# A decoder layer's weight blocks: six hand-divided places of one tile instead of a buffer for each block

## The chip, the cores and the metric

The kernel runs on one core of one Trainium2 chip. The metric is the device time of one execution in microseconds (us); below 2080.77 us is the median of three runs of the kernel as it was (2077.95 to 2080.8).

## The reference, cut to what matters

One decoder layer over 528 tokens (16 learned ones ahead of 512), all in float32, width 2048:

```python
n = rmsnorm(h, g_mix);  p = n @ w_in                  # 2048 -> 6144: q, k, v, b, c, u
o = concat(stick_breaking_attention(q, k, v), b * causal_conv(c * u))   # each group normed
h = h + o @ w_out                                     # 2048 -> 2048
n2 = rmsnorm(h, g_ffn)
h = h + (silu(n2 @ w_gate) * (n2 @ w_up)) @ w_down    # 2048 -> 5632 -> 2048
return h[:, 16:]
```

Nothing of what is computed changes. The change touches only where the weights of `w_out`, `w_gate`, `w_up` and above all `w_down` stand in the core's SBUF, and so when they are loaded.

## The kernel before, in words

**Precision.** A float32 product is made of three matmuls in the faster type `fp32r`: a weight block is split into `hi` (ACT casts it, L613) and `lo` (DVE subtracts `hi` from the block, L614), the activations likewise, and TensorE (PE) adds hi by hi (L706), hi by lo (L707) and lo by hi (L708) into one PSUM bank. One matmul is 128x128 weights by 256 tokens.

**Seven products for eight.** From the gate and up projections on, the work goes in *pairs*: a pair is a 2x2 arrangement of weight blocks `11`, `12`, `21`, `22` (two output tiles by two halves of the contraction), multiplied by a 2x2 arrangement of activation blocks with seven block products instead of eight. The weights of the seven are, in order: `11`; `t1 = 11 + 12`; `t2 = t1 + 22`; `22`; `t3 = 12 + 22`; `21`; and the final `t2 = t2 + 21`. DVE makes the sums: L620 makes t1 and t3, L654 and L627 add to t2, which stands in t1's buffer. There are 72 pairs: 44 for gate and up (0 to 43; 8 weight tiles of 128 to a block), 4 double pairs of `w_down`'s first chunk (44 to 47; again 8 tiles), and 24 pairs of `w_down`'s other three chunks (48 to 71, eight to a chunk; 6 tiles to a block, so 128x768). A pair of the last kind is 7 products of 18 matmuls, 126 in all. The activation blocks of these chunks stand in a ring of buffers that POOL's queue fills from DRAM (`ring<-fd`).

**The banks.** The products of a pair go to three PSUM banks in the order x, z, x, z, x, y, x (`pair_product`). After the fifth product DVE takes its result out of bank x (L741, into `d`), and the seventh product, which goes to bank x again, may not start before. The sixth product, to bank y, lies between: 18 matmuls for pairs 48 to 71.

**The loads.** SP's queue holds the weight loads, strictly in order; each waits until its buffer is free. Before the change each of the four blocks has one buffer of 128x1024 (`b11`, `b12`, `b21`, `b22`, L591), so `22` of pair i+1 can be loaded only when `22` of pair i has been split. Each load is issued by `load_quad(i + 1, q)` beside the last instruction that reads the same block of pair i. Two further buffers of that size serve t1 and t3 (`sum`), and three double ones hold hi and lo of the split blocks (`s`): three products are prepared at a time. All of it takes 48 KB of each partition, before the change and after it.

**The order.** The program is recorded with a scheduler that moves instructions by priority and by what they depend on; `prepare_pair` runs at high priority, ahead of the products by two. DVE, ACT and SP each work strictly in the order that it made.

Of the kernel before, what the change touches and what calls it, by code (L numbers as in the profile page):

```python
# [9 lines left out]
F32 = mybir.dt.float32  # L10
F32R = mybir.dt.float32r
# [4 lines left out]
P = 128  # L16
# [6 lines left out]
KT = D // P  # L23
FT = FF // P
# [9 lines left out]
def hybrid_layer(ctx: ExitStack, tc: tile.TileContext, xT, w_in, w_out, w_gu, w_down, vecs, out):  # L34
# [12 lines left out]
    def open_pool(name, bufs=1, **kw):  # L47
        return tc.alloc_tile_pool(name=name, bufs=bufs, reuse_waits="tile", **kw)
# [513 lines left out]
    sw = open_pool("sw", side="right")  # L562
    acc_h = hpool.tile([P, SEQ], F32, name="acc_h")
    hpool.tile([P, 24], F32, name="pad_h")
    pairs = []
# [17 lines left out]
    quads, sums, split_w, used = {}, {}, [], [0]  # L583
    S_AHEAD = 2
    ORDER = ("21", "11", "12", "22")
    WIDE = 2 * KT - 2

    def load_quad(i, q):
        if i < len(pairs):
            n, srcs = pairs[i]  # L590
            quads[i, q] = sw.tile([P, 8 * P], F32, tag=f"b{q}", name=f"b{q}_{i}")[:, : n * P]  # L591
            src, dst = srcs[("11", "12", "21", "22").index(q)], quads[i, q]
            if len(src.shape) == 3:
                dst = dst.rearrange("p (t c) -> p t c", t=2)
            nc.sync.dma_start(dst, src)

    wide = []

    def load_wide():

        i = len(wide)
        q = ORDER[(i + 2) % 4]
        if i < WIDE:
            wide.append(sw.tile([P, 8 * P], F32, tag=f"b{q}", name=f"wide{i}"))
            nc.sync.dma_start(wide[i], w_out[OUT_TILES[1 + i // 2], i % 2])
        else:
            wide.append(None)
            load_quad(0, q)

    def split_quad(src, n):  # L610
        t = sw.tile([P, 2, 8 * P], F32R, tag="s", bufs=S_AHEAD + 1, name=f"s{len(split_w)}")
        hi, lo = (t[:, i, : n * P] for i in range(2))
        sc.copy(hi, src)  # L613
        ve.tensor_tensor(lo, src, hi.bitcast(F32), ALU.subtract)  # L614
        split_w.append((hi, lo))

    def add_quads(i, name, a, b):
        n = pairs[i][0]
        sums[name] = sw.tile([P, 8 * P], F32, tag="sum", bufs=2, name=f"{name}_{i}")[:, : n * P]
        ve.tensor_tensor(sums[name], a, b, ALU.add)  # L620

    def add_t3(i, b):
        add_quads(i, "t3", b["12"], b["22"])
        load_quad(i + 1, "12")

    def add_last(i, b):
        ve.tensor_tensor(sums["t2"], sums["t2"], b["21"], ALU.add)  # L627
        load_quad(i + 1, "21")


    FIRST_ORDER = (5, 0, 1, 2, 3, 4, 6)
# [1 line left out]
    def prepare_pair():  # L633
        if len(split_w) < WIDE:
            with tc.high_priority():
                split_quad(wide[len(split_w)], 8)
                load_wide()
            return
        i, s = divmod(len(split_w) - WIDE, 7)
        if i == len(pairs):  # L640
            return
        n = pairs[i][0]
        if i == 0:
            s = FIRST_ORDER[s]
        with tc.high_priority():
            b = {q: quads[i, q] for q in ("11", "12", "21", "22") if (i, q) in quads}
            if s == 0:
                split_quad(b["11"], n)
                add_quads(i, "t1", b["11"], b["12"])
                load_quad(i + 1, "11")  # L650
            elif s == 1:
                split_quad(sums["t1"], n)
                sums["t2"] = sums["t1"]
                ve.tensor_tensor(sums["t2"], sums["t2"], b["22"], ALU.add)  # L654
                if i:
                    add_t3(i, b)
            elif s == 2:
                split_quad(sums["t2"], n)
                if not i:
                    add_t3(i, b)  # L660
            elif s == 3:
                split_quad(b["22"], n)
                load_quad(i + 1, "22")
            elif s == 4:
                split_quad(sums["t3"], n)
            elif s == 5:
                split_quad(b["21"], n)
                if i:
                    add_last(i, b)
            else:  # L670
                if not i:
                    add_last(i, b)
                split_quad(sums["t2"], n)

    def prepare_ahead(n):
        while len(split_w) < min(WIDE + 7 * len(pairs), used[0] + n):
            prepare_pair()
# [96 lines left out]
    for _ in range(4):  # L774
        load_wide()
# [11 lines left out]
    for i, j in enumerate(OUT_TILES):  # L787
# [8 lines left out]
        half, k = divmod(j, 8)  # L796
# [285 lines left out]
```

## Time and profile before

| | |
|---|---|
| median of 3 runs | 2080.77 us (2077.95 to 2080.8) |
| the profiled execution | 2082.13 us, its span 2080.4 us |
| PE busy | 2057.9 us, 99% of the span |
| VectorE (DVE) busy | 1628.2 us, 78% |
| ScalarE (ACT) busy | 1016.4 us, 49% |
| loads of `w_down` of 128x768 | 96, 384.0 KB each, median 3.9 us from issue to landing |
| loads of the activation ring, 768.0 KB | 42, median 14.1 us |
| granted TensorE clock | 0.998 of full speed on average |

A line of the profile names a line of the kernel, an engine, an operation, and what it writes and reads without buffer numbers: `t<-b,b` is a sum of two loaded blocks, `s<-b,s` a split of one, `d<-x,sides` the reading out of bank x. "Idle before" is the time in which the engine stood still ahead of an instruction, with what ended it. PE's matmuls overlap: each is shown as 0.28 us long, but the next one starts about 0.11 us later. SPq and POOLq are the queues of transfers that SP and POOL issue.

### The profile page before, as it was taken

To read this page: it belongs to the slowest core of one execution; us is meant where nothing else is said; L and a number is where in the kernel's file an instruction comes from. 1 tells how busy PE (TensorE), PEld (TensorE's weight loads), DVE (VectorE), ACT (ScalarE), POOL (GpSimd) and SP (SyncE) were. 2 spreads that over 40 slices of the span, in tenths; PEclk is the share of its full clock that TensorE was granted. 3 is DMA by queue.
4 is the path that set the end of the run, shared out by engine and by line. 5 is a ranking of instruction groups with operands and counts; after the bars stand their busy time and mean duration, and the time that the engine had idled before them with its cause. 6 is when DMAs were issued, how large, how long until landed. Compare 5 with 4: busy or idle time off the path is not lost.

```text
span 2080.4 us, 39146 instructions
## 1 busy us (share of the span) xinstructions
PE 2057.9 (99%) x16086; PEld 1983.3 (95%) x16086; DVE 1628.2 (78%) x2133; ACT 1016.4 (49%) x1522; POOL 368.3 (18%) x499
## 2 busy tenths in 40 slices
PE   9999999999999999999999999999999999999999
PEld 8899999999998888999999999999999999999999
DVE  7877777433336668999898888988988977878888
ACT  7666565322224434555555555555555554444443
POOL 0111111010003544111011011111110233131210
PEclk9999999999999999999999999999999999999999
DMA  5222222222235666546555465465555999696765
GB/s 194 63 82 73 80 72 82 85 97 93 92 112 163 186 185 224 160 139 194 155 166 164 146 174 158 137 174 166 146 171 151 290 336 340 149 334 155 206 149 110
DMA packets 144116, 330.41 MB, mean 159 GB/s; under 512 B 12400, under 2 KB 62064, under 8 KB 143936
## 3 DMA queue, kind: packets, MB, share of 16 engines
q1 hardware_dynamic: 67456, 212.50, 32.1%
q0 software_dynamic: 76480, 115.40, 21.8%
q8 instruction: 126, 2.06, 0.4%
q14 instruction: 54, 0.44, 0.1%
HBM read 260.74 MB, written 67.11 MB: 158 GB/s over the span
## 4 chain that ended last, share of the span: by engine, by line
PE 90%; DVE 4%; DMA 4%; ACT 1%; issue 1%; SPq 0%; POOL 0%; DVEq 0%; ACTq 0%; POOLq 0%
PE x L706 10%; PE x L708 10%; PE x L707 10%; PE z L706 5%; PE z L707 5%; PE z L708 5%; DMA b<-w_down 3%; PE po L685 3%; PE po L686 3%; PE po L687 3%; PE y L707 2%; PE y L708 2%; PE y L706 2%; DVE s L614 2%; PE pu L177 1%; PE pc L177 1%
## 5 line engine op out<-in xcount | busy, mean ns | idle before, releaser
L613 ACT CAST s<-t 128x1024 fp32r<-128x1024 f32 (+1 forms) x288 | 283.2, 983 | 372.8 <-PE z L708 165.6
L614 DVE TENSOR_TENSOR s<-t,s 128x1024 fp32r<-128x1024 f32 (+1 forms) x288 | 327.4, 1137 | 101.6 <-ACT s L613 99.4
L708 PE MATMUL x<-f,s 128*128 128x256 f32 x1408 | 388.2, 276 | 3.2 <-DVE s L614 3.2
L707 PE MATMUL x<-f,s 128*128 128x256 f32 x1408 | 388.3, 276 | 1.5 <-DMA f<-fx 1.3
L706 PE MATMUL x<-f,s 128*128 128x256 f32 x1408 | 388.1, 276 | 0.2 <-ACT f L187 0.2
L613 ACT CAST s<-b 128x1024 fp32r<-128x1024 f32 (+1 forms) x216 | 212.4, 983 | 159.7 <-PE x L708 141.0
L708 PEld LDWEIGHTS x<-f,s 128*128 128x128 f32 x1408 | 265.2, 188 | 3.4 <-DVE s L614 3.4
L707 PEld LDWEIGHTS x<-f,s 128*128 128x128 f32 x1408 | 265.1, 188 | 1.9 <-DMA f<-fx 1.5
L706 PEld LDWEIGHTS x<-f,s 128*128 128x128 f32 x1408 | 265.0, 188 | 0.7 <-ACT f L187 0.4
L614 DVE TENSOR_TENSOR s<-b,s 128x1024 fp32r<-128x1024 f32 (+1 forms) x216 | 245.8, 1138 | 2.6 <-ACT s L613 2.0
L142 DVE TENSOR_TENSOR wlo<-raw,whi 128x512 fp32r<-128x512 f32 (+1 forms) x198 | 139.9, 710 | 126.5 <-ACT whi L141 125.9
L898 POOL DMA_DIRECT2D fd<-s x147 | 103.7, 922 | 693.4 <-DVE s L188 676.9
L141 ACT CAST whi<-raw 128x512 fp32r<-128x512 f32 (+1 forms) x198 | 121.0, 614 | 182.3 <-PE pu L175 65.5
L706 PE MATMUL z<-f,s 128*128 128x256 f32 x704 | 193.8, 275 | 0.7 <-ACT sides L733 0.7
L707 PE MATMUL z<-f,s 128*128 128x256 f32 x704 | 193.8, 275 | 0.2 <-DVE f L188 0.2
L708 PE MATMUL z<-f,s 128*128 128x256 f32 x704 | 193.7, 275 | 0.0
L620 DVE TENSOR_TENSOR t<-b,b 128x1024 f32<-128x1024 f32 (+1 forms) x144 | 166.0, 1153 | 22.9 <-DMA b<-w_down 17.6
L706 PE MATMUL x<-ring,s 128*128 128x256 f32 x608 | 169.2, 278 | 7.8 <-DVE d L741 7.8
L708 PE MATMUL x<-ring,s 128*128 128x256 f32 x608 | 168.8, 278 | 0.5 <-DVE s L614 0.5
L707 PE MATMUL x<-ring,s 128*128 128x256 f32 x608 | 168.7, 277 | 0.0
L706 PEld LDWEIGHTS z<-f,s 128*128 128x128 f32 x704 | 132.2, 188 | 0.9 <-ACT sides L733 0.9
L707 PEld LDWEIGHTS z<-f,s 128*128 128x128 f32 x704 | 132.2, 188 | 0.4 <-DVE f L188 0.4
(349 smaller groups left out, 5581.6 us busy)
## 6 DMA issues: line engine op xcount, KB each, us to landing
b<-w_gu SPq DMA_DIRECT2D x176, 512.0 KB, 3.9
raw<-w_in SPq DMA_DIRECT2D x92, 512.0 KB, 3.3
fd<-s POOLq DMA_DIRECT2D x147, 256.0 KB, 5.3
b<-w_down SPq DMA_DIRECT2D x96, 384.0 KB, 3.9
ring<-fd POOLq DMA_DIRECT2D x42, 768.0 KB, 14.1
wide<-w_out SPq DMA_DIRECT2D x30, 512.0 KB, 3.7
out_T<-d POOLq DMA_DIRECT2D x54, 256.0 KB, 4.6
b<-w_down SPq DMA_DIRECT2D x16, 512.0 KB, 7.9
```

The costliest lines, as they stand in the source:

```text
L141: sc.copy(hi[:, :c], raw)
L142: ve.tensor_tensor(lo[:, :c], raw, hi[:, :c].bitcast(F32), ALU.subtract)
L613: sc.copy(hi, src)
L614: ve.tensor_tensor(lo, src, hi.bitcast(F32), ALU.subtract)
L620: ve.tensor_tensor(sums[name], a, b, ALU.add)
L685: pe.matmul(ps, hi[:, kk], ah, start=k == 0, stop=False)
L686: pe.matmul(ps, hi[:, kk], al, start=False, stop=False)
L687: pe.matmul(ps, lo[:, kk], ah, start=False, stop=k == 7)
L706: pe.matmul(p, hi[:, kk], act[:, 0, k], start=start and j == k == 0, stop=False, skip_group_check=skip)
L707: pe.matmul(p, hi[:, kk], act[:, 1, k], start=False, stop=False, skip_group_check=skip)
L708: pe.matmul(p, lo[:, kk], act[:, 0, k], start=False, stop=k == n - 1, skip_group_check=skip)
L898: gp.dma_start(fd[c][s][:, :, k], t[:, :, i])
```

## The change

All blocks that are loaded, and the two sums, now stand in one tile `sw_in` of 128x6144; the split blocks in a second one, `sw_split`, of the same size. Both are divided by hand.

* Where a block has 8 tiles (pairs 0 to 47) `sw_in` has six places of 128x1024: four for the blocks, two for the sums, as before.
* Where it has 6 (pairs 48 to 71) the same tile has eight places of 128x768: the sums have places 6 and 7, and the blocks go round the **six** places 0 to 5, in the order 11, 12, 22, 21 of pair 48, then 11, 12 of pair 49, and so on.
* The two sums exchange places in every second pair (`(name == "t3") ^ i % 2`): t1 of a pair takes the place that t3 of the pair before had. Before, the pool gave t1 whichever of its two buffers came free first, which was the same one.
* A load is issued when a place comes free, so it is now that of the block two further on (`load_next`). Two more loads are issued when the six places start.

For pairs 48 to 71 this is when a load may be issued, counted in instructions of DVE's order (17 to a pair):

| block | issued before, after | issued now, after | how much earlier |
|---|---|---|---|
| 22 of pair i+1 | split of 22 of pair i | split of 11 of pair i | 9 |
| 21 of pair i+1 | split of 21 of pair i | t3 of pair i | 14 |
| 11 of pair i+1 | split of 11 of pair i | split of 22 of pair i-1 | 8 |
| 12 of pair i+1 | t3 of pair i | split of 21 of pair i-1 | 3 |

First place: SP's queue, the loads for pairs 48, 49 and the first two of 50 (`b12_48` is block 12 of pair 48; a name in the waits is a counter that the load waits for, DVE's or that of an earlier load). Before:

```order
L595 DMA b12_48_18992<-w_down 128x768 [waits DMAHW2_49,DVE_49]
L595 DMA b11_48_18959<-w_down 128x768 [waits DMAHW7_49,DMAHW3_49,DVE_49]
L595 DMA b22_48_19061<-w_down 128x768 [waits DMAHW4_49,DVE_49]
L595 DMA b21_48_19120<-w_down 128x768 [waits DMAHW5_49,DVE_49]
L595 DMA b12_49_19213<-w_down 128x768 [waits DMAHW6_49,DVE_49]
L595 DMA b11_49_19180<-w_down 128x768 [waits DMAHW7_49,DVE_49]
L595 DMA b22_49_19283<-w_down 128x768 [waits DMAHW0_49,DVE_49]
L595 DMA b21_49_19330<-w_down 128x768 [waits DMAHW1_49,DVE_49]
L595 DMA b12_50_19405<-w_down 128x768 [waits DMAHW2_49,DVE_49]
L595 DMA b11_50_19378<-w_down 128x768 [waits DMAHW3_49,DVE_49]
```

and now, all of them into `sw_in`:

```order
L608 DMA sw_in_6909<-w_down 128x768 [waits DMAHW3_49,DVE_49]
L608 DMA sw_in_6909<-w_down 128x768 [waits DMAHW7_49,DMAHW2_49]
L608 DMA sw_in_6909<-w_down 128x768 [waits DMAHW4_49,DVE_49]
L608 DMA sw_in_6909<-w_down 128x768
L608 DMA sw_in_6909<-w_down 128x768 [waits DMAHW5_49,DVE_49]
L608 DMA sw_in_6909<-w_down 128x768
L608 DMA sw_in_6909<-w_down 128x768 [waits DMAHW6_49,DVE_49]
L608 DMA sw_in_6909<-w_down 128x768 [waits DMAHW7_49,DVE_49]
L608 DMA sw_in_6909<-w_down 128x768 [waits DMAHW0_49,DVE_49]
L608 DMA sw_in_6909<-w_down 128x768 [waits DMAHW1_49,DVE_49]
```

They are now 11, 12, 22, 21 of pair 48, then 12, 11, 22, 21 of pair 49, and 11, 12 of pair 50; three of the first six no longer wait for DVE on their own account, since the load ahead of them has waited for it already.

Second place: DVE where the places of 128x1024 give way to those of 128x768 (`z47` and `x47` are banks z and x of pair 47). Before:

```order
L614 TENSOR_TENSOR s363_19088<-t3_47_18990,s363_19088 128x1024
L620 TENSOR_TENSOR t1_48_19178<-b11_48_18959,b12_48_18992 128x768
L614 TENSOR_TENSOR s364_19116<-b21_47_18899,s364_19116 128x1024
L737 SCALAR_TENSOR_TENSOR d_first_18335<-z47_19028,d_first_18335 128x512
L614 TENSOR_TENSOR s365_19147<-t1_47_18957,s365_19147 128x1024
L620 TENSOR_TENSOR t3_48_19211<-b12_48_18992,b22_48_19061 128x768
L741 SCALAR_TENSOR_TENSOR d_first_18335<-x47_19029,d_first_18335 128x512
L614 TENSOR_TENSOR s366_19175<-b11_48_18959,s366_19175 128x768
L744 TENSOR_TENSOR d_first_18335<-y47_19027,sides_8227 128x512
```

and now (L637, L643, L762, L766 and L769 are the former L614, L620, L737, L741 and L744; x3 means three in a row):

```order
L637 TENSOR_TENSOR sw_split_6910<-sw_in_6909,sw_split_6910 128x1024 x3
L762 SCALAR_TENSOR_TENSOR d_first_17695<-z47_18349,d_first_17695 128x512
L637 TENSOR_TENSOR sw_split_6910<-sw_in_6909,sw_split_6910 128x1024
L643 TENSOR_TENSOR sw_in_6909<-sw_in_6909 128x768
L637 TENSOR_TENSOR sw_split_6910<-sw_in_6909,sw_split_6910 128x768
L643 TENSOR_TENSOR sw_in_6909<-sw_in_6909 128x768
L766 SCALAR_TENSOR_TENSOR d_first_17695<-x47_18350,d_first_17695 128x512
L637 TENSOR_TENSOR sw_split_6910<-sw_in_6909,sw_split_6910 128x768
L769 TENSOR_TENSOR d_first_17695<-y47_18348,sides_8161 128x512
```

The sum t1 of pair 48 stood two instructions ahead of the read-out of bank z (L737); its new place overlaps both old places of sums, so it now stands behind the last split of pair 47. Between the read-outs of bank z and bank x there were a split and a sum, and now there are two of each. From pair 49 on DVE's order is what it was.

PE's order is the same instruction for instruction, and so is POOL's. On ACT the first casts of pair 1 are exchanged (block 22 is cast one ahead of t2, since the places of the split blocks now go round in a fixed order), and in the output projection one cast of 128x256 stands behind the weights' cast instead of ahead of it; DVE's splits of these follow. Each half of a split block now has a place of its own, so 232 of the 504 splits on DVE wait for PE as well as for ACT's cast, where they waited for ACT alone (or with a load).

```diff
--- before.py
+++ after.py
@@ -585,15 +585,38 @@
     ORDER = ("21", "11", "12", "22")
     WIDE = 2 * KT - 2
 
+
+    QUADS = ("11", "12", "22", "21")
+    SIX = FT + KT // 4
+    sw_in = sw.tile([P, 6 * 8 * P], F32, name="sw_in")
+    sw_split = sw.tile([P, 6 * 8 * P], F32R, name="sw_split")
+
+    def w_place(t, n, i):
+        return t[:, i * n * P : (i + 1) * n * P]
+
+    def quad_place(i, q):
+        m = QUADS.index(q)
+        return w_place(sw_in, pairs[i][0], m if i < SIX else (4 * (i - SIX) + m) % 6)
+
     def load_quad(i, q):
         if i < len(pairs):
             n, srcs = pairs[i]
-            quads[i, q] = sw.tile([P, 8 * P], F32, tag=f"b{q}", name=f"b{q}_{i}")[:, : n * P]
+            quads[i, q] = quad_place(i, q)
             src, dst = srcs[("11", "12", "21", "22").index(q)], quads[i, q]
             if len(src.shape) == 3:
                 dst = dst.rearrange("p (t c) -> p t c", t=2)
             nc.sync.dma_start(dst, src)
 
+    def load_next(i, q):
+
+        m = QUADS.index(q)
+        if i < SIX:
+            load_quad(i + 1, q)
+            if i + 1 == SIX and m == 3:
+                load_quad(SIX + 1, QUADS[0])
+        else:
+            load_quad(i + 1 + (m + 2) // 4, QUADS[(m + 2) % 4])
+
     wide = []
 
     def load_wide():
@@ -601,31 +624,31 @@
         i = len(wide)
         q = ORDER[(i + 2) % 4]
         if i < WIDE:
-            wide.append(sw.tile([P, 8 * P], F32, tag=f"b{q}", name=f"wide{i}"))
+            wide.append(quad_place(0, q))
             nc.sync.dma_start(wide[i], w_out[OUT_TILES[1 + i // 2], i % 2])
         else:
             wide.append(None)
             load_quad(0, q)
 
     def split_quad(src, n):
-        t = sw.tile([P, 2, 8 * P], F32R, tag="s", bufs=S_AHEAD + 1, name=f"s{len(split_w)}")
-        hi, lo = (t[:, i, : n * P] for i in range(2))
+        k = len(split_w) % (S_AHEAD + 1) * 2
+        hi, lo = (w_place(sw_split, n, k + i) for i in range(2))
         sc.copy(hi, src)
         ve.tensor_tensor(lo, src, hi.bitcast(F32), ALU.subtract)
         split_w.append((hi, lo))
 
     def add_quads(i, name, a, b):
         n = pairs[i][0]
-        sums[name] = sw.tile([P, 8 * P], F32, tag="sum", bufs=2, name=f"{name}_{i}")[:, : n * P]
+        sums[name] = w_place(sw_in, n, (4 if n == 8 else 6) + ((name == "t3") ^ i % 2))
         ve.tensor_tensor(sums[name], a, b, ALU.add)
 
     def add_t3(i, b):
         add_quads(i, "t3", b["12"], b["22"])
-        load_quad(i + 1, "12")
+        load_next(i, "12")
 
     def add_last(i, b):
         ve.tensor_tensor(sums["t2"], sums["t2"], b["21"], ALU.add)
-        load_quad(i + 1, "21")
+        load_next(i, "21")
 
 
     FIRST_ORDER = (5, 0, 1, 2, 3, 4, 6)
@@ -647,7 +670,7 @@
             if s == 0:
                 split_quad(b["11"], n)
                 add_quads(i, "t1", b["11"], b["12"])
-                load_quad(i + 1, "11")
+                load_next(i, "11")
             elif s == 1:
                 split_quad(sums["t1"], n)
                 sums["t2"] = sums["t1"]
@@ -660,7 +683,7 @@
                     add_t3(i, b)
             elif s == 3:
                 split_quad(b["22"], n)
-                load_quad(i + 1, "22")
+                load_next(i, "22")
             elif s == 4:
                 split_quad(sums["t3"], n)
             elif s == 5:
@@ -671,6 +694,8 @@
                 if not i:
                     add_last(i, b)
                 split_quad(sums["t2"], n)
+                if i + 1 == SIX:
+                    load_quad(SIX + 1, QUADS[1])
 
     def prepare_ahead(n):
         while len(split_w) < min(WIDE + 7 * len(pairs), used[0] + n):
```

## The prediction

> **What bounds the kernel now.** I read the page's busy shares first, then who PE waits for.
>
> ```profile
> span 2080.4 us, 39146 instructions
> PE 2057.9 (99%) x16086; PEld 1983.3 (95%) x16086; DVE 1628.2 (78%) x2133; ACT 1016.4 (49%) x1522; POOL 368.3 (18%) x499
> ...
> PE x L706 <- DVE d L741: 7.8, 5, 2.7
> PE x L708 <- DVE s L614: 3.7, 2, 3.2
> ```
>
> PE works through the whole span, so only its pace and its waits count. By far the longest sum of waits is the one for L741, the read-out of bank x: five times, 7.8 us. PE's timeline shows where they are, with the first matmul of pair 48, the first of pair 66 and the last of pair 71 beside them:
>
> ```profile
> 1721.29 0.28 PE L706 MATMUL x<-ring,s 128*128 128x256 f32 x1
> ...
> 1748.77 0.36 PE L706 MATMUL x<-ring,s 128*128 128x256 f32 x1 [0.80 <-DVE d L741]
> ...
> 1764.50 0.35 PE L706 MATMUL x<-ring,s 128*128 128x256 f32 x1 [1.16 <-DVE d L741]
> ...
> 1838.06 0.36 PE L706 MATMUL x<-ring,s 128*128 128x256 f32 x1 [1.87 <-DVE d L741]
> ...
> 1869.87 0.35 PE L706 MATMUL x<-ring,s 128*128 128x256 f32 x1 [1.34 <-DVE d L741]
> ...
> 1958.52 0.55 PE L706 MATMUL x<-ring,s 128*128 128x256 f32 x1 [2.68 <-DVE d L741]
> ...
> 1990.73 0.28 PE L706 MATMUL x<-ring,s 128*128 128x256 f32 x1
> ...
> 2076.30 0.28 PE L708 MATMUL x<-ring,s 128*128 128x256 f32 x1
> ```
>
> All five lie in pairs 48 to 71, the very pairs for which the change adds places. What this stage loses follows from counts. The last six pairs have 6 x 126 = 756 matmuls, 755 intervals in 2076.30 - 1990.73 = 85.57 us: 0.1133 us each, 14.28 us a pair. All 24 pairs have 3023 intervals, 342.6 us at that pace; they took 2076.30 - 1721.29 = 355.0 us. **12.4 us** are lost.
>
> DVE's timeline and the chain of waits say to what. In the chain's rows (start, length) the load's start is its issue and its end its landing:
>
> ```profile
> 1820.94 0.95 DVE L614 TENSOR_TENSOR s<-b,s 128x768 fp32r<-128x768 f32 x1
> ...
> 1827.99 0.95 DVE L614 TENSOR_TENSOR s<-b,s 128x768 fp32r<-128x768 f32 x1
> ...
> 1833.02 0.96 DVE L614 TENSOR_TENSOR s<-t,s 128x768 fp32r<-128x768 f32 x1 [0.39 <-ACT s L613]
> 1836.62 0.96 DVE L620 TENSOR_TENSOR t<-b,b 128x768 f32<-128x768 f32 x1 [2.65 <-DMA b<-w_down]
> 1837.49 0.42 DVE L741 SCALAR_TENSOR_TENSOR d<-x,sides 128x256 f32<-128x256 f32 x1
> ...
> 1740.89 6.34 DMA b<-w_down
> 1756.58 6.39 DMA b<-w_down
> 1828.97 7.55 DMA b<-w_down
> 1861.83 6.51 DMA b<-w_down
> 1948.62 8.36 DMA b<-w_down
> ...
> DVE t L620 <- DMA b<-w_down: 14.3, 9, 3.5
> DMA to landing us min/median/max: 3.0/3.3/9.3
> ```
>
> Take the third stall. The split of block 22 of pair 55 ends at 1828.94; block 22 of pair 56 is issued at 1828.97 into its buffer and lands at 1836.52. The sum t3 = 12 + 22 stood ready to start at 1833.98, when the split ahead of it ended, and waits 2.65 us for it. L741 needs nothing of that load, but stands behind the sum in DVE's order, and PE's seventh product behind L741. So the load had 5.0 us, and where the ring's transfers run beside it it takes 6.3 to 8.4. All five PE stalls follow one of these five loads. The median of 3.3 us shows why the other pairs do not stall.
>
> A part of the 12.4 us comes after the stalls:
>
> ```profile
> core 0: us, PE busy (x) PEld busy (x) DVE busy (x) ACT busy (x) POOL busy (x), PEclk, DMA share, GB/s
> 1793.00:1807.00 14.00, 14.00 (x126) 14.00 (x125) 12.45 (x18) 6.65 (x10) 1.71 (x2) 1.00 0.68 152
> 1836.00:1852.00 16.00, 14.13 (x110) 13.97 (x109) 12.78 (x17) 5.82 (x9) 6.13 (x8) 0.89 1.14 374
> ...
> 1839.08 0.42 PE L707 MATMUL x<-ring,s 128*128 128x256 f32 x1
> ```
>
> The waits as shown sum to 7.85 us; PE's matmuls overlap, so from one start to the next each costs 0.28 - 0.11 = 0.16 us more, 8.7 us for five. The other 3.7 us are matmuls at half clock behind the two long stalls (0.42 us long instead of 0.28, granted clock 0.89 over the 16 us around the one; 0.11 x 16 = 1.8 us of clock missing, twice at the most) and slightly slow ones behind each stall.
>
> [...]
>
> **The change part by part.**
>
> *The loads ahead.* Block 22 is now issued behind the split of block 11 of the pair before, which ends at 1821.89 in the rows above: 7.1 us before 1828.97. It has 12.1 us until its sum instead of 5.0. The longest landing in this stage is 9.3 us. The other blocks had more time already (11 instructions of DVE or more against 6) and get more. So L620 waits for no load here, L741 is on time, and the stalls go with their half clock: -12.4 us. Bounds: -12.4 is all that the stage loses, no more can be gained; if under the ring's transfers landings grew beyond 12.1 us for the worst two, the stalls of 1.87 and 2.68 would stay with their clock, and -12.4 would be -5. I take the whole, since a grown landing must add 2.8 us to the longest seen. PE's next limit is its own pace, which no edit touches.
>
> *The seam at pair 47.* Here two more instructions stand ahead of the read-out of bank x.
>
> ```profile
> 1715.68 0.96 DVE L620 TENSOR_TENSOR t<-b,b 128x768 f32<-128x768 f32 x1
> 1716.56 0.68 DVE L741 SCALAR_TENSOR_TENSOR d_first<-x,d_first 128x512 f32<-128x512 f32 x1
> 1717.16 0.95 DVE L614 TENSOR_TENSOR s<-b,s 128x768 fp32r<-128x768 f32 x1
> ...
> 1716.05 0.84 ACT L613 CAST s<-b 128x768 fp32r<-128x768 f32 x1 [1.66 <-PE x L708]
> 1718.57 0.28 PE L706 MATMUL x<-first,s 128*128 128x256 f32 x1
> ```
>
> The split now ahead of it waits for ACT's cast, which ends at 1716.89; t1 takes DVE's time from 1715.68 to 1716.64 in the meantime. Then the split to 1717.9, t3 to 1718.8, L741 (0.68) to 1719.5. PE wants bank x at 1718.57, so it stalls about **+0.9 us**, once. Bounds 0 (if PE runs late there) and +1.6 (its wait is under 1.87, so I count no clock, but a load that lands late at the seam would add to it; 0.7 is room for that).
>
> *The exchanged sums and fixed rounds.* t1 of the next pair keeps the place that came free, so DVE's order from pair 49 on is the old one: 0. Had it a fixed place, t1 would wait for the last split.
>
> *232 more waits on DVE.* The place that a split's lo half goes to was last read by PE before ACT's cast could begin, so PE is done long before. If one did end last, it would cost the 0.10 us that lie between the landing at 1836.52 and L620 at 1836.62. Cover is DVE's idle time: 14.0 - 12.45 = 1.5 us in 14 us of a quiet stretch, and 1.75 to 2.2 in a gate pair of 19.05:
>
> ```profile
> 1200.00:1219.05 19.05, 19.05 (x171) 19.05 (x170) 16.81 (x20) 9.71 (x13) 4.22 (x6) 1.00 0.82 216
> 1219.05:1238.10 19.05, 19.05 (x171) 19.05 (x170) 17.29 (x21) 10.25 (x13) 1.16 (x3) 1.00 0.32 103
> ```
>
> Seven in a pair are 0.7 us at the most: 0. Without that cover 232 x 0.10 = +23 us.
>
> *Casts and splits exchanged* at pair 1 and in the output projection: one cast and one split ahead of another, 0.98 + 1.14 = 2.1 us by the page's rows, under a product of 24 matmuls, 2.72 us:
>
> ```profile
> L613 ACT CAST s<-t 128x1024 fp32r<-128x1024 f32 (+1 forms) x288 | 283.2, 983 | 372.8 <-PE z L708 165.6
> L614 DVE TENSOR_TENSOR s<-t,s 128x1024 fp32r<-128x1024 f32 (+1 forms) x288 | 327.4, 1137 | 101.6 <-ACT s L613 99.4
> ```
>
> I take 0, with -1 to +1 for it.
>
> *Sum.* -12.4 + 0.9 = -11.5. The profiled execution took 2082.13 us (span 2080.4 and 1.7 around it): 2070.6. It lies 1.4 above the median of the runs shown, 2080.77, from which the same gain gives 2069.3. I predict **2070 us**.
>
> **The rivals.**
>
> 1. *The ring comes late instead.* Weight loads issued earlier share the transfer engines with the ring's transfers, and PE, no longer held up, reaches the ring's blocks sooner. For it: 374 GB/s in the window around the third stall. Against: the list of PE's waits has no row for the ring, the bytes are the same, and most of a chunk's ring blocks are loaded several pairs ahead. Price: the two long stalls' worth comes back at the chunk seams, half the gain: 2070 + 6 = 2076. [...]
> 2. *The change does not do what it says*: an SP queue in strict order could hold an early load behind one whose place is not free. In the table of issues the places come free in the queue's order (splits of 21, t3, splits of 11, splits of 22 in turn), which speaks against it. Then the stalls stay and the seam is added: 2080.8 + 0.9 = 2081.7.
> 3. *Slower: DVE's added waits.* For it: 232 of them, on the engine whose lateness stalls PE today. Against: the idle time quoted. It decides once seven of them use up DVE's 1.5 us in a pair, 0.2 us each; if all their 23 us fell on the path, 2070 + 23 = 2093.
>
> **How the numbers follow.** The forecast has 74%; the ring 12%; no effect 8%; DVE's waits 6%. Its own range is 2066 (the fastest run of before, 2077.95, less 12.4) to 2074 (seam +1.6, casts +1, a short stall left). The range of 8 in 10 takes in the ring and ends short of no effect: 2066 to 2077.5. This kernel can be told from no change by about 0.2%, 4.2 us, so faster means under 2076.6: the forecast and two thirds of the ring's case, 0.82; same, the rest of the ring's and most of no effect, 0.11; slower, DVE's waits and the tail of no effect, 0.07.
>
> **What would show it.** Right: in pairs 48 to 71 no wait of PE for the read-out of bank x except one of about 0.8 us as shown, at the end of pair 47; no wait of the sums for `w_down` over 0.2 us; first to last matmul of these pairs 343 us; no window there with a granted clock under 1.00. Wrong: PE waits named after the ring's transfers (rival 1), sums still waiting for loads issued no earlier than today (rival 2), splits on DVE that PE ends (rival 3). A pace other than 0.1133 us per matmul in these pairs, from weights at other addresses, would make the whole sum wrong, and no row here prices that.

## The result and the profile after

The changed kernel takes 2065.91 us (median of 4 runs, 2065.38 to 2068.78), the kernel before 2079.36 us on the same chip (2075.76 to 2080.8): ratio **0.9939**, 95% interval 0.9926 to 0.9952, that is 13.5 us less by the medians. The forecast was 2070. The profiled execution took 2065.55 us.

The page of the changed kernel, and the list of what PE waits for (us in total, times, longest), from its top row to the one row left for the read-out of bank x (L766, the former L741):

```profile
span 2063.9 us, 39364 instructions
PE 2050.4 (99%) x16086; PEld 1977.2 (96%) x16086; DVE 1629.1 (79%) x2133; ACT 1017.7 (49%) x1522; POOL 368.8 (18%) x499
...
PE x L733 <- DVE sw_split L637: 2.2, 2, 1.7
...
PE x L731 <- DVE d_first L766: 0.3, 1, 0.3
```

The row of 7.8 us is gone. PE's timeline at the seam of pair 47, the first matmul of pair 48 and the last of pair 71:

```profile
1713.73 0.28 PE L733 MATMUL y<-first,sw_split 128*128 128x256 f32 x1
1714.29 0.35 PE L731 MATMUL x<-first,sw_split 128*128 128x256 f32 x1 [0.28 <-DVE d_first L766]
...
1717.12 0.28 PE L731 MATMUL x<-ring,sw_split 128*128 128x256 f32 x1
...
2059.73 0.28 PE L733 MATMUL x<-ring,sw_split 128*128 128x256 f32 x1
```

Pairs 48 to 71 take 2059.73 - 1717.12 = **342.61 us** instead of 355.01: 12.40 us less, PE's pace from end to end. DVE's timeline at the place of the former third stall, the windows of the whole stage and around that place, and the waits and landings of the blocks:

```profile
1827.19 0.96 DVE L643 TENSOR_TENSOR sw_in<-sw_in 128x768 f32<-128x768 f32 x1
1828.07 0.42 DVE L766 SCALAR_TENSOR_TENSOR d<-x,sides 128x256 f32<-128x256 f32 x1
```

```profile
core 0: us, PE busy (x) PEld busy (x) DVE busy (x) ACT busy (x) POOL busy (x), PEclk, DMA share, GB/s
1717.12:2059.80 342.68, 342.68 (x3026) 342.68 (x3024) 302.01 (x404) 158.23 (x239) 63.80 (x78) 1.00 0.80 213
1826.00:1842.00 16.00, 16.00 (x143) 16.00 (x142) 14.22 (x19) 7.19 (x12) 6.12 (x8) 1.00 1.12 374
```

```profile
DVE sw_in L643 <- DMA sw_in<-w_down: 0.8, 2, 0.5
...
DMA to landing us min/median/max: 3.0/4.0/10.1
```

The transfers are as dense as before (374 GB/s) and the slowest load even slower, 10.1 us from issue to landing (9.3 before). No sum notices: t3 runs without a wait and L766 right behind it. The two waits of 0.8 us together lie ahead of pair 48.

The 16.57 us between the last matmuls (2076.30 and 2059.73) are 12.40 of this stage and 4.17 ahead of it. The 4.17 add up from four places: 1.36 won in the program's first 14 us, far ahead of the part that the change touches; 1.07 lost near 802 us, where the changed kernel waits longer for activations; 4.4 won from there to 833 us, in pairs 0 and 1; and 0.5 lost between pairs 1 and 48, of which 0.44 is the seam. Most of the 4.4 belongs to one wait: the third matmul (lo by hi) of pair 1's first product waited 1.5 us longer before than after, and 1.6 us were lost at half clock behind it (3.41 us from 821.63 us on). PE's timeline of the kernel before, and then of the changed one:

```profile
820.15 0.38 PE L708 MATMUL x<-f,s 128*128 128x256 f32 x1 [3.25 <-DVE s L614]
```

```profile
817.19 0.39 PE L733 MATMUL x<-f,sw_split 128*128 128x256 f32 x1 [1.74 <-DVE sw_split L637]
```

Ahead of the split that PE waited for stands the sum t3 of pair 1, which waited 1.77 us for a load of gate weights before and 0.57 us in the changed kernel. The forecast gives pairs 0 and 1 no more than 1 us either way; how far the difference belongs to the change is taken up after the experiments.

### The profile page after: what moved, and what is told of

It is laid out like the page before. It is cut to its first block, busy times and chain, and to the rows that moved or that the text cites. A ratio compares the mean times of both kernels' runs of the same rounds, so it can differ in the third digit from the quotient of the medians.

```text
span 2063.9 us, 39364 instructions
## 1 busy us (share of the span) xinstructions
PE 2050.4 (99%) x16086; PEld 1977.2 (96%) x16086; DVE 1629.1 (79%) x2133; ACT 1017.7 (49%) x1522; POOL 368.8 (18%) x499
## 4 chain that ended last, share of the span: by engine, by line
PE 96%; DVE 2%; DMA 1%; ACT 0%; issue 0%; SPq 0%; POOL 0%; DVEq 0%; ACTq 0%; POOLq 0%
PE x L733 11%; PE x L731 11%; PE x L732 11%; PE z L731 6%; PE z L732 6%; PE z L733 6%; PE y L733 3%; PE y L731 3%; PE y L732 3%; PE po L712 3%; PE po L710 3%; PE po L711 3%; PE pu L177 2%; PE pc L177 2%; PE pv L173 2%; PE pu L173 1%
## 5 line engine op out<-in xcount | busy, mean ns | idle before, releaser
L636 ACT CAST sw_split<-sw_in 128x1024 fp32r<-128x1024 f32 (+1 forms) x534 | 527.0, 989 | 552.4 <-PE z L732 166.7
L637 DVE TENSOR_TENSOR sw_split<-sw_in,sw_split 128x1024 fp32r<-128x1024 f32 (+1 forms) x534 | 615.0, 1152 | 96.9 <-ACT sw_split L636 94.0
L733 PE MATMUL x<-f,sw_split 128*128 128x256 f32 x1408 | 387.3, 275 | 1.7 <-DVE sw_split L637 1.7
L732 PE MATMUL x<-f,sw_split 128*128 128x256 f32 x1408 | 387.3, 275 | 1.3 <-DVE f L188 1.3
L731 PE MATMUL x<-f,sw_split 128*128 128x256 f32 x1408 | 387.2, 275 | 0.2 <-ACT f L187 0.2
L733 PEld LDWEIGHTS x<-f,sw_split 128*128 128x128 f32 x1408 | 264.3, 188 | 1.9 <-DVE sw_split L637 1.9
L732 PEld LDWEIGHTS x<-f,sw_split 128*128 128x128 f32 x1408 | 264.3, 188 | 1.5 <-DVE f L188 1.5
L731 PEld LDWEIGHTS x<-f,sw_split 128*128 128x128 f32 x1408 | 264.3, 188 | 0.5 <-ACT f L187 0.4
L731 PE MATMUL z<-f,sw_split 128*128 128x256 f32 x704 | 193.7, 275 | 0.6 <-ACT sides L758 0.6
L732 PE MATMUL z<-f,sw_split 128*128 128x256 f32 x704 | 193.6, 275 | 0.0
L733 PE MATMUL z<-f,sw_split 128*128 128x256 f32 x704 | 193.6, 275 | 0.0
L643 DVE TENSOR_TENSOR sw_in<-sw_in 128x1024 f32<-128x1024 f32 (+1 forms) x144 | 165.9, 1152 | 5.4 <-DMA sw_in<-w_down 0.8
L733 PE MATMUL x<-ring,sw_split 128*128 128x256 f32 x608 | 167.3, 275 | 0.5 <-DVE sw_split L637 0.5
L731 PE MATMUL x<-ring,sw_split 128*128 128x256 f32 x608 | 167.2, 275 | 0.0
L732 PE MATMUL x<-ring,sw_split 128*128 128x256 f32 x608 | 167.2, 275 | 0.0
L731 PEld LDWEIGHTS z<-f,sw_split 128*128 128x128 f32 x704 | 132.2, 188 | 0.8 <-ACT sides L758 0.8
L733 PEld LDWEIGHTS z<-f,sw_split 128*128 128x128 f32 x704 | 132.2, 188 | 0.0
L732 PEld LDWEIGHTS z<-f,sw_split 128*128 128x128 f32 x704 | 132.2, 188 | 0.0
L733 PEld LDWEIGHTS x<-ring,sw_split 128*128 128x128 f32 x608 | 114.1, 188 | 0.7 <-DVE sw_split L637 0.7
```

The source lines that it names most:

```text
L731: pe.matmul(p, hi[:, kk], act[:, 0, k], start=start and j == k == 0, stop=False, skip_group_check=skip)
L732: pe.matmul(p, hi[:, kk], act[:, 1, k], start=False, stop=False, skip_group_check=skip)
L733: pe.matmul(p, lo[:, kk], act[:, 0, k], start=False, stop=k == n - 1, skip_group_check=skip)
```

## The experiments

The theory is the forecast's: block 22 had 5.0 us from issue to its sum, late landings held up the sum t3, t3 held up the read-out of bank x, and the read-out held up PE. A kernel's line numbers are its own.

**Four places again.** The hand-divided tile stays; its blocks of six tiles go back to four places and the old times of issue.

```diff
-        return w_place(sw_in, pairs[i][0], m if i < SIX else (4 * (i - SIX) + m) % 6)
+        return w_place(sw_in, pairs[i][0], m)
...
-        if i < SIX:
-            load_quad(i + 1, q)
...
-            load_quad(i + 1 + (m + 2) // 4, QUADS[(m + 2) % 4])
+        load_quad(i + 1, q)
...
```

> The changed kernel with one thing undone: in pairs 48 to 71 the blocks of six tiles keep four places (as before the change) and a load is issued one block ahead, so block 22 of the next pair again has about 5 us until its sum. The hand-divided tiles, the waits on DVE, the exchanged casts of pair 1 and the exchange of the sums' places stay. Theory (the gain of these pairs is the earlier loads and nothing else): they take about 355 us from first to last matmul again instead of 342.6 (350 to 358, since which loads land late varies), with PE waits for the read-out of bank x behind loads of w_down; time about 2078, ratio to the changed kernel +0.6%. Rival (the gain comes from the tiles or the sums' places): they stay near 343 us and the time near 2066. The 4.6 us won at pairs 0 and 1 that the forecast did not have: if they come from the exchanged casts and the fixed places, the stall of 3.5 us with its half clock near 820 us stays away here (stall of 2 us or less); if they are chance of the loads, either may be seen.

Measured: 2077.11 us, ratio to the kernel before 0.9993 (0.9983 to 1.0003). First and last matmul of the stage, and PE's and DVE's waits:

```profile
1717.80 0.28 PE L724 MATMUL x<-ring,sw_split 128*128 128x256 f32 x1
...
2069.83 0.28 PE L726 MATMUL x<-ring,sw_split 128*128 128x256 f32 x1
```

```profile
PE x L724 <- DVE d L759: 6.4, 5, 1.6
```

```profile
DVE sw_in L638 <- DMA sw_in<-w_down: 15.7, 12, 2.5
```

352.0 us: the waits are back (a sixth, of 1.3 us at the same kind of matmul, is put down to ACT's cast), and with them 9.4 of the 12.4 us; the last section says where the other 3 are. The tile, the waits that it adds on DVE, the exchanged casts and the exchanged sums are all in this kernel, so the gain is the earlier issue alone, and rival 3 falls.

**Block 22 loaded twice**, with the kernel before and with the changed one: the suspected landing time, doubled.

```diff
             nc.sync.dma_start(dst, src)
+            if q == "22" and i >= len(pairs) - 23:
+                nc.sync.dma_start(dst, src)
```

> The kernel before with block 22 of pairs 49 to 71 loaded twice into its buffer, the second time when the first has landed; t3's sum waits for the second. Only SP's queue gets instructions, 23 of 0.33 us; the orders of the engines stay. Theory (PE's stall is block 22's time from issue to landing less about 5.6 us): two quiet landings of 3.0 to 3.3 us make 6.0 to 6.6, a PE wait of 0.4 to 1.0 us for the read-out of bank x in nearly every one of the 23 pairs, and several us in the five or so where the ring's transfers run beside: pairs 48 to 71 take 375 to 420 us instead of 355. Rival (the stalls belong to something else than this landing): about 355 us.

> The changed kernel with the same second loads of block 22 for pairs 49 to 71. Theory (12.1 us from issue to the sum): the quiet pairs (6.0 to 6.6 us) show nothing; only where both landings are long (over 12 us together, two to four pairs) a PE wait is left, and SP's queue, which stands during the second wait, holds no other block beyond its time. Pairs 48 to 71 take 343 to 352 us. Rival (the earlier issue is worth no more than a few us, or SP's standing queue delays the other blocks): over 360 us.

Measured: 2141.56 us with the kernel before (ratio 1.0312, 1.0275 to 1.0349), 2078.77 us with the changed one (1.0009, 0.9995 to 1.0022; both against the kernel before). With the kernel before: first and last matmul of the stage, PE's waits, and the chain at one quiet pair:

```profile
1721.85 0.28 PE L708 MATMUL x<-ring,s 128*128 128x256 f32 x1
...
2138.63 0.28 PE L710 MATMUL x<-ring,s 128*128 128x256 f32 x1
```

```profile
PE x L708 <- DVE d L743: 35.7, 15, 8.7
```

```profile
1788.17 3.06 DMA b<-w_down
...
1791.24 3.26 DMA b<-w_down
...
1794.60 0.96 DVE t L622
1795.56 0.33 DVE d L743
```

With the changed kernel the same two rows of PE, its waits, and the chain at one of the pairs that still stall:

```profile
1719.25 0.28 PE L733 MATMUL x<-ring,sw_split 128*128 128x256 f32 x1
...
2071.06 0.28 PE L735 MATMUL x<-ring,sw_split 128*128 128x256 f32 x1
```

```profile
PE x L733 <- DVE d L768: 6.6, 4, 2.4
```

```profile
1731.54 8.20 DMA sw_in<-w_down
...
1739.76 6.21 DMA sw_in<-w_down
```

416.8 us against 351.8, both inside the ranges written down. The row of 15 waits is not all of it with the kernel before: six more stalls at the first matmul of a seventh product are put down to ACT's cast (4.4 us) or to nothing that the profile shows (12.3 us). In all 21 of the 24 pairs stall there, and the granted clock of the whole execution is 0.988, where the runs of the kernel before beside it have 0.998 to 1.0. In the quiet pair two landings of 3.1 and 3.3 us are enough to hold up the sum (by 1.75 us), the read-out and PE. The changed kernel shows nothing of such pairs; five of its pairs stall. The pair shown in it needs 8.20 + 6.21 = 14.4 us, and its sum then waited 2.46 us: a window of about 12 us, as the forecast counted it. The same added bytes cost 61.8 us without the places and 9.2 with them.

**The sum behind the read-out.** The kernel before, its buffers and loads untouched; the edit only turns round DVE's order of two instructions.

```diff
-                    add_t3(i, b)
+                    with tc.issue_after(read_x[0].ins):
+                        add_t3(i, b)
...
-        ve.scalar_tensor_tensor(c2[:, 1], x, -1.0, p5, ALU.mult, ALU.subtract)
+        read_x[0] = ve.scalar_tensor_tensor(c2[:, 1], x, -1.0, p5, ALU.mult, ALU.subtract)
...
```

> The kernel before, its buffers and loads as they were, with one thing moved: the sum t3 stands behind the read-out of bank x in DVE's order instead of ahead of it. Theory (PE was stalled because that read-out, which needs nothing of the load, stood behind a sum that waited for one): the sums still wait for loads of w_down, but the read-out does not, so PE's five waits for it go; pairs 48 to 71 take 343 to 346 us instead of 355, and the time is about 2069 to 2072. What is late next is the split of t3, needed two products later (4 us), so nothing of it reaches PE unless a load lands more than about 9 us after its issue. Rival (a late load stalls PE whatever stands behind it): PE waits as long, for splits of t3 instead of the read-out, and the pairs stay near 355 us, 2080.

Measured: 2069.32 us, ratio 0.9959 (0.9946 to 0.9972); the stage takes 347.35 us. PE's waits in it, DVE's for loads, and ACT's timeline ahead of one of PE's:

```profile
PE x L708 <- ACT sides L733: 2.8, 5, 0.8
```

```profile
DVE t L620 <- DMA b<-w_down: 12.2, 11, 1.9
```

```profile
1834.05 0.84 ACT L613 CAST s<-t 128x768 fp32r<-128x768 f32 x1 [4.07 <-DVE t L655]
1834.79 0.82 ACT L613 CAST s<-b 128x768 fp32r<-128x768 f32 x1
1835.52 0.36 ACT L733 COPY sides<-x 128x256 f32<-128x256 f32 x1
```

The sums still wait 12.2 us for loads, and no wait for the read-out is left: that a sum stood ahead of it was the link. 7.7 of the 12.4 us are won without any new place. Not all, and not the 343 to 346 expected: five shorter waits stand elsewhere, which neither theory named. The late sum puts off DVE's next sums (L655); ACT's casts wait for L655, the copy of the side bank (L733) stands behind these casts, and PE waits for that copy. The delay went from one strictly ordered engine to the next.

**The seam, and both edits together.** First the parity of the exchange is turned over in the changed kernel; then t3 is moved as above too.

```diff
-... + ((name == "t3") ^ i % 2))
+... + ((name == "t1") ^ i % 2))
```

> The changed kernel with the parity of the sums' exchange turned over: t1 of pair 48 then stands in a place that overlaps only the old place of t3 of pair 47, which is free early, so the sum and the split that stand ahead of the read-out of bank x at the seam go back to where they were. Theory (the seam's cost is the two more instructions of DVE ahead of that read-out): PE's wait for it at the end of pair 47 (0.3 us as shown, 0.44 from start to start) is gone, pairs 48 to 71 stay at 342.6 us, and the time is 0.4 us less than the changed kernel's, too little to be told by the timing. Rival (the seam's wait comes from elsewhere, such as a late load): it stays.

> Both edits on the changed kernel: the sums' parity turned over and t3 behind the read-out of bank x in every pair. Theory: in pairs 48 to 71 nothing is left to win but the 0.4 us of the seam. In pairs 0 to 47 a late load of t3 no longer holds the read-out up; of the 2.0 us that PE waits in pair 1 at 815 us up to 2 us can go. Time 2063 to 2066. Rival (t3's own split then comes late, since the sum now follows the read-out): PE waits for splits of t3, some 0.1 to 1 us a pair in the gate pairs, where DVE is idle for only 1.75 us of 19.05: 5 to 40 us slower.

Measured: 2067.24 us (ratio to the kernel before 0.9946, 0.9935 to 0.9958) and 2066.75 us (0.9946, 0.9934 to 0.9958). In both the stage takes 342.61 us and PE's wait at the seam is gone. DVE's timeline there, with the parity alone:

```profile
1713.80 0.96 DVE L643 TENSOR_TENSOR sw_in<-sw_in 128x768 f32<-128x768 f32 x1
1714.68 0.95 DVE L637 TENSOR_TENSOR sw_split<-sw_in,sw_split 128x768 fp32r<-128x768 f32 x1
1715.55 0.68 DVE L766 SCALAR_TENSOR_TENSOR d_first<-x,d_first 128x512 f32<-128x512 f32 x1
```

The sum t1 left its place between the read-outs; a split ahead of L766 stayed, and DVE is in time all the same. The 0.44 us are real and cannot be told in the time: neither version is faster than the change as it is (2065.91). The 2 us hoped for at pair 1 did not come, and 2066.75 lies above the 2063 to 2066 expected: with t3 behind the read-out PE waits there 2.1 us for the activations (`f<-fx`) instead.

**No exchange at all.** t1 always in the one place, t3 in the other.

```diff
-... + ((name == "t3") ^ i % 2))
+... + (name == "t3"))
```

> The changed kernel without the exchange of the sums' places: t1 has always the one place, t3 the other. Then t1 of a pair may be made only when the last split of the pair before is done, and the seam of pair 47, where DVE does two more instructions ahead of the read-out of bank x, is there in every pair. Theory (the forecast put the exchange at 0 and said that with a fixed place t1 would wait): PE waits for the read-out of bank x in nearly every pair, by some 0.5 to 0.9 us in the gate pairs and about 1.2 us in pairs 48 to 71; 30 to 70 us slower than the changed kernel, 2095 to 2135. Rival (the scheduler puts t1 behind the read-out, or DVE's idle time takes it): within 5 us of 2066. Pairs 0 and 1 have the changed kernel's order of casts: if that order is what won 4.6 us there, the stall near 815 us is again about 2 us.

Measured: 2082.55 us, ratio to the kernel before 1.0021 (1.0010 to 1.0032). The longest sums of waits, of DVE for loads and of PE:

```profile
DVE sw_in L643 <- DMA sw_in<-w_down: 18.4, 5, 5.7
```

```profile
PE y L733 <- DVE sw_split L637: 6.5, 4, 2.0
```

Some 17 us lost, below the range, and not where the theory had them. Pairs 48 to 71 take 343.0 us, pairs 2 to 42 only 0.7 us more: there t1 waits for the last split, but the scheduler puts t3, whose place is free early, into t1's old position, and t1 takes t3's, ahead of the read-out. The two swap at almost no cost. The loss is at pair 1 (PE stands 5.0 us from start to start), in pair 43 (2.6 us) and in pairs 44 to 47 (77.7 us in the changed kernel, 87.5 here). What is lost at pair 1 need not be the edit's: the time of that region, 48.6 us, lies inside what other kernels show there (below). The rows show sums waiting for loads of `w_down` there, up to 5.7 us, and splits queued behind them; that it is t3, now made earlier, meeting block 22 not yet landed follows from the order and was not tested apart. So the exchange is worth its line, and mostly in other pairs than was expected.

**More traffic, in two attempts that only half worked.** First, copies that nobody reads on POOL's queue.

```diff
+            if c < len(CHUNKS) - 1 or j < KT // 2 - 2:
+                for e in range(2):
+                    aside = dram.tile([P, 2, CHUNKS[c], T2], F32R, name=f"aside{c}_{j}_{e}")
+                    for part in range(2):
+                        gp.dma_start(aside[:, part], fd[c][e][:, part], max_dma_last_dim=3072)
```

> The kernel before, with two more copies from DRAM to DRAM (768 KB each in two halves, read by nobody) on POOL's queue in nearly every pair of w_down's last three chunks, to make the loads of w_down land late as the ring's transfers do. Theory (PE's stalls are the landing time of block 22 less the 5.0 us that it has): landings of 6 to 9 us in most of the pairs that carry copies and with each a PE wait of 1 to 3 us for the read-out of bank x: pairs 48 to 71 take 370 to 410 us instead of 355. Rival (the stalls are something else's, for instance of the seams of chunks): they stay at five or so and the stage near 355 us. Pairs 0 and 1 are untouched here, so this is a second look at them in the kernel before: if its order of casts makes the stall of 3.5 us with half clock near 817 us, it is here again; if it was chance, some 2 us are seen as in the changed kernel.

> The changed kernel with the same added copies. Theory (a block has 12.1 us until its sum): under the same late landings pairs 48 to 71 stay at 343 to 346 us, as long as no load lands more than 12 us after its issue. Rival (the forecast's first: the ring comes late where the transfer engines are loaded more): PE waits named after the ring's transfers or L643 waiting for loads, stage over 350 us. Pairs 0 and 1 are again as in the changed kernel: a stall of about 2 us near 815 us if its order makes it so, up to 3.5 us if it is chance.

Measured: 2107.74 us (ratio 1.0132, 1.0103 to 1.0162) and 2101.81 us (1.0104, 1.0074 to 1.0133); the stage 375.4 and 366.6 us. The forecast for the changed kernel was missed, and for a reason that makes both runs poor tests: the copies need only `fd`, so the scheduler moved them ahead, into the gate pairs and the first of the three chunks (the last are issued at 1807 and 1810 us), and the kernel's own stores of `d` stood behind them on POOL's queue. The row of DVE in the changed kernel with copies:

```profile
DVE d L762 <- DMA out_T<-d: 14.7, 4, 7.4
```

Pairs 56 to 71 come after the last copy and so say nothing of added traffic: they take 228.4 us in the changed kernel with copies, as without (2059.73 - 1831.36 = 228.4), and 236.7 in the kernel before with copies, 234.9 without (2076.30 - 1841.43). One thing of rival 1 does show: with copies on the ring's own queue PE waited once for a ring transfer in pair 48, 2.5 us in the changed kernel and 1.1 us in the kernel before.

Second, ACT issues the copies, in its own strict order.

```diff
...
+        with tc.issue_after(last_cast[0].ins):
+            for m in range(2):
+                src = pairs[k][1][m]
+                aside = dram.tile(list(src.shape), F32, name=f"aside{i}_{m}")
+                sc.dma_start(aside, src)
...
```

> The kernel before with two copies of 512 KB from DRAM to DRAM (blocks of the gate weights, read by nobody) issued by ACT in each of pairs 48 to 69, the first right behind the cast of block 22, so that they run beside the load of the next block 22. Unlike the copies on POOL's queue, nothing of the kernel stands behind them on their queue, and ACT's strict order keeps them in their pair. PE's stalls of the kernel before were about the landing time less 5.6 us (6.34 us: 0.80; 7.55 us: 1.87). Theory: landings of block 22 go to 6 to 8 us in most of the 22 pairs, each with a PE wait of 0.5 to 2.5 us for the read-out of bank x; pairs 48 to 71 take 370 to 400 us instead of 355, by t3's sums waiting for w_down. Rival (the stalls belong to something else than these landings): still five or so, near 355 us. Pairs 0 and 1 are untouched, a third look at them in the kernel before.

> The changed kernel with the same copies in the same places. Theory (12.1 us from issue to the sum): the same landings of 6 to 9 us reach nothing; pairs 48 to 71 stay at 342.6 to 344 us, no sum waits over 0.3 us for w_down. Rival (the forecast's first, the ring comes late when the transfer engines are loaded): PE waits named after ring transfers, over 350 us. Pairs 0 and 1 are untouched, one more look at them in the changed kernel.

Measured: 2108.84 us (1.0139, 1.0092 to 1.0187) and 2101.31 us (1.0103, 1.0058 to 1.0148); the stage 382.3 and 375.8 us. Again the changed kernel's 343 was missed. PE's waits in the changed kernel with these copies:

```profile
PE x L744 <- ACT sides L769: 25.0, 22, 1.1
```

With a DMA issue behind the cast, a further cast came to stand ahead of the copy of the side bank on ACT, and in every one of the 22 pairs PE stood 1.41 us from start to start (1.52 with the kernel before). What can be read beside it: in this stage the sums of the kernel before waited 13.0 us for `w_down`, 14 times; those of the changed kernel never. The clean test is the double load above.

## Why the forecast was right, point by point

* **The time**: 2065.91 us is 4.1 us under the forecast, at the lower end of its range, 2066 (worked out as 2077.95 - 12.4 = 2065.55). The median of before is now 2079.36 instead of 2080.77, which is 1.4 of it, and the seam was taken 0.5 too large; the rest is within the scatter, since the interval of the gain, 10.0 to 15.4 us, contains the sum of 11.5.
* **The loads ahead, -12.4**: 12.40 measured. Shown, not only argued: four places bring the stalls back, and the doubled landing shows windows of about 5 and 12 us. The slowest load, 10.1 us, fits. The bound of -5 does not come out of the forecast's own rows: the two long stalls lengthened pairs 55, 56, 63 and 64 to 17.64, 14.70, 18.71 and 14.31 us instead of 14.28; had they stayed, 8.2 us would be lost still and 4.2 won. No other number rests on it.
* **The seam, +0.9**: mis-sized, 0.44 (0.3 as shown). The two instructions stand where the forecast put them. The term that failed is ACT's cast, which the forecast took from the kernel before, ending 1.68 us ahead of PE's wish for bank x (1716.89 and 1718.57). ACT's timeline in the changed kernel:

```profile
1710.53 0.84 ACT L636 CAST sw_split<-sw_in 128x768 fp32r<-128x768 f32 x1 [0.98 <-PE x L732]
```

It ends at 1711.37, and PE wished for the bank at 1713.85 (1714.29 less 0.44): 2.48 us ahead. The cast's place comes free 0.8 us earlier, so the split ahead of L766 waits for no cast. In the forecast that wait held the split from 1716.64 to 1716.99.
* **The exchanged sums, 0**: right for the change. That t1 would wait with a fixed place was right too; what this was expected to cost ahead of that run (some 1.2 us in each of pairs 48 to 71) was not: 0.4 us in all of pairs 48 to 71, 10 us in pairs 44 to 47.
* **232 waits on DVE, 0**: right; the version with four places has them all and is no slower than the kernel before (0.9993), and from pair 2 to pair 47 the changed kernel keeps the old time to 0.5 us.
* **Casts and splits exchanged at pair 1, 0 within 1**: here the profiled runs differ by 4.4 us in the change's favour, more than the range of this term. Most of it is scatter from one execution to the next. The same 340 matmuls from 803 us on took, in four kernels with the old order, 47.6, 43.2, 48.9 and 47.8 us, and in six with the new one 43.1, 43.1, 46.1, 45.8, 47.3 and 45.4. The old order had 43.2 once and the new one 47.3, by when the loads of gate weights and activations land (the sum's 1.77 and 0.57 us above; PE's wait for `f<-fx`, 1.31 us at 813.77 us in the kernel before, none named in the changed kernel). Left out are the three kernels that change the order of the sums themselves; they lie in the same span (42.7, 45.0 and 48.6 us). Whether 1 or 2 us of the mean (46.9 against 45.1) belong to the change stays open. With the 1.36 us of the program's start it is much of why the profiled pair (16.6 us) shows more than the medians (13.5).
* **Rivals**: the ring late (no PE wait is named after it in the changed kernel, at the same 374 GB/s; only the two kernels with copies on the ring's own queue show one, of 1.1 and 2.5 us), no effect, and DVE's added waits (above): none of them is seen here.

## What to carry to other kernels

Look at what stands *behind* a wait on a strictly ordered engine: the five late loads cost 12.4 us only because a read-out that needed none of them was queued after the sum that did. There are two cures, an earlier issue (a place more for the load, all 12.4 us) or another order (a few lines, 7.7 us), and after either one it must be asked which queue the delay goes to next. When an edit seems to gain in a region that it hardly touches, look at the same region in several other runs before giving it a cause.

## What the runs showed of the hardware beside it

Half clock did not go by a stall's length alone. The granted clock in the profiles of the kernel before and of the changed one knows only full and half. In the kernel before, up to its last matmul, three stretches of half begin at 821.63, 1838.80 and 1958.27 us; each lasts 3.413 us, and 298 and 35 times that lie between their starts (1017.17 and 119.47 us), as on a fixed grid. The changed kernel has none until 2063.12 us, behind its last matmul. Around the third stall of the kernel before, cut on that grid:

```profile
1835.42:1838.83 3.41, 1.54 (x13) 1.37 (x13) 2.21 (x4) 0.83 (x1) 0.00 (x0) 1.00 1.14 403
1838.83:1842.25 3.42, 3.42 (x18) 3.42 (x17) 3.35 (x6) 0.10 (x1) 1.65 (x2) 0.51 1.17 405
1842.25:1845.66 3.41, 3.41 (x32) 3.41 (x31) 2.69 (x4) 1.83 (x3) 2.98 (x5) 1.00 1.11 335
```

and near 817 us of the changed kernel with copies on POOL's queue, where PE stood 3.47 us from start to start, longer, cut into stretches of the same length:

```profile
813.50:816.90 3.40, 2.03 (x18) 1.83 (x17) 2.11 (x1) 1.36 (x2) 3.28 (x4) 1.00 0.63 186
816.90:820.30 3.40, 1.57 (x13) 1.57 (x14) 3.40 (x5) 0.00 (x0) 2.83 (x2) 1.00 0.99 376
820.30:823.70 3.40, 3.40 (x32) 3.40 (x32) 3.37 (x4) 1.32 (x2) 0.00 (x0) 1.00 0.45 145
```

The 2.15 us of the first cost a window at half clock, the 3.47 us of the second none; that the second lay across two windows is an estimate from its first two rows, with 18 and 13 matmuls. Counted by matmuls started in a window at full clock, 30 or 31 where nothing waits, from 800 us on: in the kernel before the windows with 12, 11 and 7 were followed by half clock, and none of those with 16 or more up to the last matmul; in the changed kernel (its grid taken from 2063.12 us) the fewest ahead of the last matmul's window is 13, and full clock followed. So by these counts the limit lies near 12 of 30 matmuls, an estimate of 40% of a window. For the forecast it means that some 3 of the 12.4 us hung on where two stalls fell in the grid: the two windows at half clock in this stage lost 1.6 us each, and in the version with four places no clock was lost (mean granted clock 1.000), and its stalls cost 9.4 us.
